# A third staging tile, the last pair's queries copied half by half, and the end of a unit issued behind the next unit's first scores, in a fused transformer block

## The chip, the cores and the metric

The kernel runs on one core of one Trainium2 chip. The metric is the device time of one execution in microseconds (us). The profile adds one execution seen by the hardware profiler: its engines are TensorE (PE), VectorE (DVE), ScalarE (ACT), GpSimd (POOL) and SyncE (SP), which issues the DMAs.

## The reference

One block of a streaming encoder, for 1024 tokens of width 1024, in float32. Heads have 64 columns; group A has 8 query heads over 2 key and value heads, group B has 8 heads of its own.

```
n = rms_norm(x); qa, ka, va, qb, kb, vb = split(n @ w_in)
ya = mixer_a(qa, ka, va)   # window of 3 chunks of 64, ALiBi, learned sinks
yb = mixer_b(qb, kb, vb)   # own chunk and 8 chunks before it, learned relative bias
h  = x + concat(rms_norm(ya), rms_norm(yb)) @ w_out
h  = h + relu(rms_norm(h) @ w_ff1)**2 @ w_ff2      # inner width 4096
out = rms_norm(h)
```

In mixer_b a token's scores are softmaxed over the keys of its band, and the softmax is multiplied by the values:

```
scores = einsum('bnqhd,bnshd->bnhqs', qc, kb) * HEAD_DIM ** -0.5 + bias
out = einsum('bnhqs,bnshd->bnqhd', softmax(where(valid, scores, -inf)), vb)
```

## The kernel before, in words

**Numbers.** Every float32 operand of a large product is kept as two pieces: a high part, a copy rounded to a shorter format by ScalarE, and a low part, the difference (`split_l`, L172, on VectorE or GpSimd). `mm3` multiplies high by high, high by low and low by high: three matmuls for one product (L166 is the matmul's line in the profile).

**Order.** Matmuls run in the order in which the code issues them: `pe` (L131) chains each to the one before. The other engines and SP each run their instructions in one fixed order too, but that one is set by a scheduler when the program is built, from what it estimates. A change of buffers or code can so move rows on ACT, DVE, POOL and SP. Every DMA that matters here is issued by SP, one after the other; an SP row that waits for its source holds all rows behind it.

**Buffers.** The pool `main` has three rings: 34 pages ("pg", `NPAGES`, 128 x 1024 float32 each), three weight stages ("ws") and two staging tiles ("tst", also 128 x 1024). Pages hold split weights, keys, queries, values, gated rows and later the operands of the MLP. A tile that is asked for waits until the earlier user of its buffer is done.

**Group B.** For each of four pairs of heads (j = 0 to 3) keys (kB), queries (qB) and values (vB) are projected, each in two halves of 512 tokens (t = 0, 1). `keys_b` (L391) handles keys and queries: VectorE scales the accumulator into the low tile `t1_..` (L398 queries, L400 keys), ScalarE casts the high tile `t0_..` (L401), GpSimd makes the low part in place (L172). Only after the second half the whole rows of both tiles, the high one first, are copied by DMA into the key pages KkB (L413, eight copies) and the query pages QqB (L410, four). High and low tile are one buffer of "tst" each, so with two buffers one projection fills the ring. `values_b` (L415) stages the values in "tst" as well (for the last pair in a page), splits them into two float16 pieces and transposes these by DMA (L446).

A `UnitB(pair, s, t)` is one head s of a pair for half the tokens, four blocks of 128. `first` holds its four scores: matmuls of QqB by KkB into `S_B`, a VectorE pass that adds the bias and finds the maximum `nm_B` (L607 for wide blocks, L609 for narrow), ScalarE's exponential (L610). Two blocks at a time then become float16 pieces `H_B` (ScalarE L850, VectorE L855) and are transposed by DMA into `G_B` (L858). `second` holds its products of `G_B` and the values into `av_B`; with the last of them `apply` (L868) adds the two halves of the accumulator, which hold the products of the values' two pieces, into `Y` (ScalarE L890, VectorE L891), and `finish` splits, squares and stores the result, gated by a power of two.

`interleave_b` (L1000) mixes one unit's products with the scores of a unit two further on (`LOOK_AHEAD`), and with steps of the `Filler` (L944): the projections of the next pair, or, at the end, `out_proj_a`. For the last pair `in_proj_halves` (L477) alternates queries and values by halves (q, v, q, v) and starts `out_proj_a` after the first two.

`out_proj_a` (L1015) multiplies group A's gated rows by w_out for eight blocks of tokens. `load_ya` (L928) loads a gated row `y0_m` (m = 0 to 3: one of four pairs of heads, first half of the tokens; L930) and splits it (ScalarE L897, VectorE L900). A block's result goes through a "tst" tile `o` (ScalarE L1039), is scaled there, and GpSimd adds it to the residual `h` that a DMA loads (L1040, L1026). Its steps are what TensorE does between the scores of the last pair.

**The MLP.** Both products use seven products of sums of quarter blocks in place of eight. Combinations of weights (T) are made by VectorE, cast by ScalarE (L1257) and split by GpSimd or VectorE into pages W; results are squared (L1307 Relu, L1308 Square) and stored. Tiles `k`, `v` and some rows come from "tst" too.

Of the kernel before, what the change touches and what calls it, by code (L numbers as in the profile page):

```python
# [8 lines left out]
F32 = mybir.dt.float32  # L9
# [19 lines left out]
BIG = 3e38  # L29
QA0, KA0, VA0, QB0, KB0, VB0 = 0, 512, 640, 768, 1280, 1792  # L30
WITH = ["", "", "k", "qv", "k", "qv", "k", "qv"]
NPAGES = 34
LOW_COLS = 256
GQ = 2
AHEAD1 = 2
# [18 lines left out]
def kernel(  # L54
# [288 lines left out]
    def place(acc, kind, name, dst, t, low_engine, st=None, rest=None):  # L343
        if kind == "v" and name != "vA":
            return values_b(acc, name, dst, t)
        if name[1] == "B":
            return keys_b(acc, kind, name, dst, t, low_engine)
        if st is not None:
            pass
        elif name == "vA":  # L350
            st = page([P, 2, HALF], f"ts_{name}_{t}")
        else:
            st = main.tile([P, 2, HALF], F32R, tag="tst", bufs=2, name=f"ts_{name}_{t}")
        c = slice(t * HALF, (t + 1) * HALF)
        if kind == "v":
            nc.vector.tensor_tensor(f(st[:, 0]), acc, R1[:, c], ALU.mult)
            return lambda *where: turn_v(st, name, dst, t, *where)
        if kind[0] == "q":
            nc.vector.scalar_tensor_tensor(f(st[:, 1]), acc, HD**-0.5, R1[:, c], ALU.mult, ALU.mult)
        else:  # L360
            nc.vector.tensor_tensor(f(st[:, 1]), acc, R1[:, c], ALU.mult)
        nc.scalar.activation(st[:, 0], f(st[:, 1]), AF.Copy)
        split_l(low_engine, st[:, 1], f(st[:, 1]), st[:, 0])

        def copies(heads):
            for hl in range(2):
                for s in heads:
                    src = f(st[s * HD : (s + 1) * HD, hl])
                    if kind == "q":
                        last = nc.sync.dma_start(f(dst[s][hl * HD : (hl + 1) * HD, c]), src)  # L370
                    else:
                        for rep in range(2):
                            last = nc.sync.dma_start(f(dst[2 * hl + s][rep * HD : (rep + 1) * HD, c]), src)
            return last.ins.name

        if rest is None:
            return copies(range(2))
        rest.append(lambda: copies((1,)))
        return copies((0,))
# [11 lines left out]
    def keys_b(acc, kind, name, dst, t, low_engine):  # L391

        if t == 0:
            halves[name] = [main.tile([P, SEQ], F32R, tag="tst", bufs=2, name=f"t{hl}_{name}") for hl in range(2)]
        c = slice(t * HALF, (t + 1) * HALF)
        hi, lo = (v[:, c] for v in halves[name])
        if kind == "q":
            nc.vector.scalar_tensor_tensor(f(lo), acc, HD**-0.5, R1[:, c], ALU.mult, ALU.mult)  # L398
        else:
            nc.vector.tensor_tensor(f(lo), acc, R1[:, c], ALU.mult)  # L400
        nc.scalar.activation(hi, f(lo), AF.Copy)  # L401
        split_l(low_engine, lo, f(lo), hi)
        if t == 0:
            return
        dst.extend(new_q(name) if kind == "q" else new_k(name))
        for hl, v in enumerate(halves[name]):
            for s in range(2):
                src = f(v[s * HD : (s + 1) * HD])
                if kind == "q":
                    nc.sync.dma_start(f(dst[s][hl * HD : (hl + 1) * HD]), src)  # L410
                else:
                    for rep in range(2):
                        nc.sync.dma_start(f(dst[2 * hl + s][rep * HD : (rep + 1) * HD]), src)  # L413

    def values_b(acc, name, dst, t):  # L415

        if t == 0:
            if name == "vB3":
                halves[name] = page([P, 2, HALF], f"ts_{name}", F32)
            else:  # L420
                halves[name] = main.tile([P, 2, HALF], F32, tag="tst", bufs=2, name=f"ts_{name}")
        st = halves[name]
        nc.vector.tensor_tensor(st[:, t], acc, R1[:, t * HALF : (t + 1) * HALF], ALU.mult)
        if t == 0:
            return
        st = st.rearrange("p a b -> p (a b)")
        top, e, up, down = (small.tile([P, 1], F32, tag=f"v{i}", bufs=2, name=f"{i}_{name}") for i in ("top", "e", "up", "down"))
        nc.vector.tensor_reduce(top, st, mybir.AxisListType.X, ALU.max, apply_absolute_value=True)
        nc.vector.tensor_scalar(top, top, 2.0**-90, None, ALU.max)
        nc.vector.tensor_scalar(e.bitcast(I32), top.bitcast(I32), 0xFF << 23, None, ALU.bitwise_and)  # L430
        nc.vector.tensor_scalar(
            up.bitcast(I32), e.bitcast(I32), -1.0, float((254 + V_UP) << 23), ALU.mult, ALU.add
        )
        nc.vector.tensor_scalar(
            down.bitcast(I32), e.bitcast(I32), 1.0, -float((V_UP + P_UP) << 23), ALU.mult, ALU.add
        )
        m = 4 + int(name[2:])
        gain = small.tile([P, 1], F32, tag="vgain", bufs=2, name=f"gain_{name}")
        nc.vector.tensor_tensor(gain, down, ogc[:, m : m + 1], ALU.mult)
        pieces = page([P, 2, SEQ], f"h{name}", F16)  # L440
        nc.scalar.activation(pieces[:, 0], st, AF.Copy, scale=up)
        nc.vector.scalar_tensor_tensor(pieces[:, 1], st, up, pieces[:, 0], ALU.mult, ALU.subtract)
        V = page([P, TB, 2, 2, HD], f"V{name}", F16)
        for s in range(2):
            for hl in range(2):
                nc.sync.dma_start_transpose(V[:, :, s, hl], pieces[s * HD : (s + 1) * HD, hl])  # L446
        dst.extend([V, down, gain])
# [341 lines left out]
            if self.i0 % 4 == 2:  # L789
                p.finish(self.i0 // 4)  # L790

    defer, pairs_b = [], []

    class UnitB:

# [72 lines left out]
        def apply(self, kb):  # L868
# [17 lines left out]
                    )  # L886
            if not last:
                return
            y = p.rows(self.t)[self.s * HD : (self.s + 1) * HD]
            nc.scalar.activation(y, self.av[HD:], AF.Copy)  # L890
            nc.vector.tensor_tensor(y, self.av[:HD], y, ALU.add)  # L891
# [108 lines left out]
    def interleave_b(unit, nexts, n_fill):  # L1000
# [3 lines left out]
        events = [(lead + (1 - lead) * r / rows, 1, r) for r in range(rows)]  # L1004
        events += [(NEXT_STEP[rows] * n, 0, n) for n in range(len(nexts))]
        spent = 0.0
        for at, kind, n in sorted(events):
            fill.steps(n_fill * (at - spent))
            spent = at
            (unit.second if kind else nexts)[n]()  # L1010
        fill.steps(n_fill * (1 - spent))
        while defer and not todo:
            defer.pop(0)[1]()

    def out_proj_a():  # L1015
# [5 lines left out]
        for tb in range(TB):  # L1021
# [6 lines left out]
            for n in range(8):  # L1028
# [6 lines left out]
                if last:  # L1035
                    yield
                if q == 3:
                    o = main.tile([P, HALF], F32, tag="tst", bufs=2, name=f"o{tb}_{dh}")
                    nc.scalar.activation(o, ps[dh], AF.Copy, scale=rA[:, tb : tb + 1])  # L1039
                    nc.gpsimd.tensor_tensor(h[:, c], h[:, c], o, ALU.add)  # L1040
                if not last:
# [68 lines left out]
        return mp.tile(shape, dt, tag="pg2", bufs=10, name=name)  # L1110

    def tst(shape, name):
        return main.tile(shape, F32, tag="tst", bufs=2, name=name)

    def pair_psum(name):
        return mps.tile([P, 2, HALF], F32, tag="ab", bufs=3, name=name)
# [19 lines left out]
    def rows2(tb):  # L1136
# [7 lines left out]
        nc.scalar.activation(h, ps, AF.Copy)  # L1144
        nc.sync.dma_start(hB[tb // 2][:, tb % 2], h)
        if tb % 4 < 2:
            rows[tb] = main.tile([P, 2, HALF], F32, tag="tst", bufs=2, name=f"n2_{tb}")
        else:
            rows[tb] = page([P, 2, HALF], f"n2_{tb}", F32)
        nc.vector.scalar_tensor_tensor(flat(rows[tb]), ps, r, g2b, ALU.mult, ALU.mult)  # L1150
# [510 lines left out]
```

## Time and profile before

| | |
|---|---|
| median of 3 runs | 1057.02 us (1054.84 to 1060.68) |
| the profiled execution | 1059.24 us |
| its span | 1057.5 us |
| mean granted TensorE clock | 0.990 |
| TensorE busy | 1024.0 us (97%) |
| VectorE, ScalarE, GpSimd busy | 700.8, 583.0, 425.0 us |
| moved by DMA | 183.77 MB |

Times of rows count from the start of the span. A row of the timeline gives the start, how long the group was busy, the engine, the source line, the instruction, the tile written and (after `<-`) the tiles read, their shape, and how many were taken together; in brackets stands how long the engine had been idle ahead, and what ended that. Tile names lose their numbers in the profile: `t_kB` is the high or the low tile of any pair. A stretch of a window row gives the window, its length, busy time and count by engine (PE, PE's weight loads, DVE, ACT, POOL), the granted clock, the mean busy share of the 16 DMA engines and GB/s. For SP a row's length is the time in which it issued.

By stages: the first projections and group A up to about 160, group B from there to 388, with the out-projection of group A among the last pair, and the MLP from about 450 to 1050, in which TensorE does not pause.

### The profile page before, as it was taken

To read this page: it belongs to the slowest core of one execution; us is meant where nothing else is said; L and a number is where in the kernel's file an instruction comes from. 1 tells how busy PE (TensorE), PEld (TensorE's weight loads), DVE (VectorE), ACT (ScalarE), POOL (GpSimd) and SP (SyncE) were. 2 spreads that over 40 slices of the span, in tenths; PEclk is the share of its full clock that TensorE was granted. 3 is DMA by queue.
4 is the path that set the end of the run, shared out by engine and by line. 5 is a ranking of instruction groups with operands and counts; after the bars stand their busy time and mean duration, and the time that the engine had idled before them with its cause. 6 is when DMAs were issued, how large, how long until landed. Compare 5 with 4: busy or idle time off the path is not lost.

```text
span 1057.5 us, 13848 instructions
## 1 busy us (share of the span) xinstructions
PE 1024.0 (97%) x4803; PEld 832.1 (79%) x4803; DVE 700.8 (66%) x1063; ACT 583.0 (55%) x969; POOL 425.0 (40%) x327
## 2 busy tenths in 40 slices
PE   9999998999958999999999999999999999999997
PEld 7888787767645768888888888888888888888886
DVE  6577677757674825795644535446869777678667
ACT  8666666756575756675554554455533333333347
POOL 0467565232461473306455444445015024024025
PEclk9999999999998999999999999999999999999999
DMA  9953537999999893315444534517997545533004
GB/s 358 261 149 91 134 86 172 193 209 201 200 257 213 177 312 116 120 55 177 170 140 155 182 117 145 194 60 257 371 393 264 168 127 170 177 124 100 1 1 159
DMA packets 141253, 183.77 MB, mean 174 GB/s; under 512 B 77952, under 2 KB 95360, under 8 KB 141184
## 3 DMA queue, kind: packets, MB, share of 16 engines
q1 hardware_dynamic: 141040, 182.63, 58.3%
q8 instruction: 38, 0.62, 0.2%
q14 instruction: 31, 0.25, 0.1%
q10 hardware_dynamic: 144, 0.26, 0.1%
HBM read 103.17 MB, written 42.99 MB: 138 GB/s over the span
## 4 chain that ended last, share of the span: by engine, by line
PE 56%; DVE 1%; ACT 0%; issue 0%; ACTq 0%
PE f L166 27%; PE f_a L166 16%; PE f_c L166 8%; PE f_b L166 4%; PE end L166 0%; DVE X L172 0%; DVE T L1235 0%; DVE k L1306 0%; ACT fo L147 0%; DVE S L1199 0%; DVE S L1206 0%; ACT uf L147 0%; DVE wf L147 0%; ACT C L147 0%; DVE S L1198 0%
## 5 line engine op out<-in xcount | busy, mean ns | idle before, releaser
L166 PE MATMUL f<-X,W 128*128 128x512 f32 x1344 | 305.8, 389 | 0.2 <-DVE X L172 0.2
L166 PEld LDWEIGHTS f<-X,W 128*128 128x128 f32 x1344 | 252.0, 188 | 52.8 <-DVE X L172 0.6
L166 PE MATMUL f_a<-V,U 128*128 128x512 f32 x756 | 173.5, 389 | 0.0
L172 POOL TENSOR_TENSOR U<-u,U 128x1024 fp32r<-128x1024 f32 x32 | 80.1, 2502 | 226.2 <-PE f_c L166 136.6
L166 PEld LDWEIGHTS f_a<-V,U 128*128 128x128 f32 x756 | 141.8, 188 | 29.7 <-DVE C L1550 0.3
L172 POOL TENSOR_TENSOR W<-T,W 128x1024 fp32r<-128x1024 f32 x29 | 77.0, 2655 | 122.9 <-ACT W L1257 122.9
L166 PE MATMUL f_c<-V,U 128*128 128x512 f32 x384 | 88.4, 389 | 0.0
L166 PEld LDWEIGHTS f_c<-V,U 128*128 128x128 f32 x384 | 72.1, 188 | 15.0
L1257 ACT ACTIVATE V<-Z 128x1024 fp32r<-128x1024 f32 x32 | 33.9, 1060 | 90.0 <-PE f_a L166 44.6
L172 POOL TENSOR_TENSOR W<-w,W 128x1024 fp32r<-128x1024 f32 x23 | 59.2, 2574 | 45.4 <-ACT W L1257 26.3
L1257 ACT ACTIVATE V<-w 128x1024 fp32r<-128x1024 f32 x24 | 25.4, 1060 | 79.3 <-issue 34.3
L1306 DVE TENSOR_TENSOR k<-f,k 128x1024 f32<-128x1024 f32 x24 | 29.3, 1222 | 60.0 <-PE f L166 60.0
L610 ACT ACTIVATE P_B<-P_B,nm_B 128x640 f32<-128x640 f32 (+2 forms) x64 | 44.3, 692 | 43.5 <-DVE nm_B L607 19.7
L1257 ACT ACTIVATE U<-u 128x1024 fp32r<-128x1024 f32 x56 | 58.5, 1045 | 11.8 <-DMA ud<-k 7.4
L172 DVE TENSOR_TENSOR V<-w,V 128x1024 fp32r<-128x1024 f32 x24 | 45.4, 1893 | 27.5 <-ACT V L1257 27.5
L855 DVE SCALAR_TENSOR_TENSOR H_B<-P_B,rc_B,H_B 128x640 f16<-128x640 f32 (+2 forms) x64 | 50.5, 813 | 17.4 <-ACT H_B L850 16.9
L166 PE MATMUL ip_qB<-nT,w_qB 128*128 128x512 f32 x192 | 56.4, 422 | 3.4 <-DVE t_qB L398 2.5
L166 PE MATMUL op_A<-w_o,y 128*128 128x512 f32 x192 | 57.4, 427 | 2.2 <-ACT o L1039 2.2
L166 PE MATMUL S_B<-KkB,QqB 128*128 128x320 f32 (+2 forms) x192 | 42.3, 330 | 15.5 <-DMA QqB<-t_qB 9.9
L166 PE MATMUL ip_kB<-nT,w_kB 128*128 128x512 f32 x192 | 53.5, 404 | 0.0
L1257 ACT ACTIVATE W<-w 128x1024 fp32r<-128x1024 f32 x24 | 25.3, 1059 | 47.4 <-PE f L166 25.4
L166 PE MATMUL ip_vB<-nT,w_vB 128*128 128x512 f32 x192 | 51.2, 400 | 0.0
(242 smaller groups left out, 1936.5 us busy)
## 6 DMA issues: line engine op xcount, KB each, us to landing
w<-in_w_ff_dram SPq DMA_DIRECT2D x64, 512.0 KB, 4.6
u<-ud SPq DMA_DIRECT2D x56, 512.0 KB, 4.3
ud<-k SPq DMA_DIRECT2D x48, 512.0 KB, 4.7
KkB<-t_kB SPq DMA_DIRECT2D x32, 256.0 KB, 4.7
xr<-in_x_dram SPq DMA_DIRECT2D x8, 512.0 KB, 9.1
QqB<-t_qB SPq DMA_DIRECT2D x16, 256.0 KB, 4.8
st_o<-in_w_out_dram SPq DMA_DIRECT2D x8, 512.0 KB, 5.5
h<-in_x_dram SPq DMA_DIRECT2D x8, 512.0 KB, 4.7
```

Source lines behind the costliest of these rows:

```text
L166: pe(nc.tensor.matmul(*args, **kw))
L172: return engine.tensor_tensor(lo, full, f(hi), ALU.subtract)
L610: nc.scalar.activation(pr, pr, AF.Exp, bias=nm, scale=-1.0, accum_out=sm)
L855: nc.vector.scalar_tensor_tensor(lo, q, rc, hi, ALU.mult, ALU.subtract)
L1257: nc.scalar.activation(w[0], full, AF.Copy)
L1306: dve.tensor_tensor(v, ps, v, ALU.add)
```

## The change

Five things are edited. The page ring shrinks from 34 to 33, and the staging ring grows from two tiles to three. In `keys_b` the low tile is asked for ahead of the high one, and its copies stand first. For the last pair's queries alone (qB3) each half is copied as soon as it is split: four copies of 64 x 512 after t = 0 and four after t = 1, in place of four of 64 x 1024. The closing steps of a unit of group B (ScalarE's and VectorE's `Y`, `finish`) move from `apply` to a new `end`, which `interleave_b` calls behind the first event of the next call, the first score of a coming unit; for the last unit, with its own last product.

```diff
-NPAGES = 34
+NPAGES = 33
+TST = 3
...
         if t == 0:
-            halves[name] = [main.tile([P, SEQ], F32R, tag="tst", bufs=2, name=f"t{hl}_{name}") for hl in range(2)]
+            halves[name] = [main.tile([P, SEQ], F32R, tag="tst", bufs=TST, name=f"t{hl}_{name}") for hl in (1, 0)]
         c = slice(t * HALF, (t + 1) * HALF)
-        hi, lo = (v[:, c] for v in halves[name])
+        lo, hi = (v[:, c] for v in halves[name])
...
-        if t == 0:
-            return
-        dst.extend(new_q(name) if kind == "q" else new_k(name))
-        for hl, v in enumerate(halves[name]):
+        split = name == "qB3"
+        if t == 0 or not split:
+            if t == 0 and not split:
+                return
+            dst.extend(new_q(name) if kind == "q" else new_k(name))
+        c = c if split else slice(0, SEQ)
+        for hl, v in zip((1, 0), halves[name]):
             for s in range(2):
-                src = f(v[s * HD : (s + 1) * HD])
+                src = f(v[s * HD : (s + 1) * HD, c])
                 if kind == "q":
-                    nc.sync.dma_start(f(dst[s][hl * HD : (hl + 1) * HD]), src)
+                    nc.sync.dma_start(f(dst[s][hl * HD : (hl + 1) * HD, c]), src)
...
             if not last:
                 return
+            ends.append(self.end)
+
+        def end(self):
+            p = self.pair
             y = p.rows(self.t)[self.s * HD : (self.s + 1) * HD]
...
-        for at, kind, n in sorted(events):
+        for k, (at, kind, n) in enumerate(sorted(events)):
             fill.steps(n_fill * (at - spent))
             spent = at
             (unit.second if kind else nexts)[n]()
+            if ends and (k == 0 or unit is units[-1][0] and k == len(events) - 1):
+                ends.pop()()
```

The other lines of the diff replace `bufs=2` by `bufs=TST` where "tst" is asked for. Code behind the first edit moves down by 1 to 10 lines (L172 becomes L173, L410 L414, L858 L862, L930 L938).

TensorE's order is the same before and after. On SP, from the keys of the last pair to the probabilities of unit B5_1 (head 5, second half of the tokens), before (G_B5_0 is a transpose of that unit's probabilities, y0_m a load of a gated row, st_om of a part of w_out):

```order
L413 DMA KkB32_3219<-t1_kB3_3132 64x1024 x2
L413 DMA KkB33_3220<-t1_kB3_3132 64x1024 x2
L858 DMA_TRANSPOSE G_B5_0_3165<-H_B5_0_3_3243 128x14x128
...
L858 DMA_TRANSPOSE G_B4_1_3276<-H_B4_1_1_3314 128x20x128
...
L930 DMA y0_2_3420<-ya_87 128x512
L122 DMA st_o4_4157<-in_w_out_dram 128x1024
L858 DMA_TRANSPOSE G_B4_1_3276<-H_B4_1_3_3365 128x20x128
L930 DMA y0_3_3434<-ya_87 128x512
L122 DMA st_o5_4171<-in_w_out_dram 128x1024
L410 DMA QqB30_3517<-t0_qB3_3301 64x1024
...
L858 DMA_TRANSPOSE G_B5_1_3445<-H_B5_1_1_3476 128x20x128
```

and after:

```order
L414 DMA QqB30_3306<-t1_qB3_3301 64x512
L414 DMA QqB31_3307<-t1_qB3_3301 64x512
L414 DMA QqB30_3306<-t0_qB3_3302 64x512
L414 DMA QqB31_3307<-t0_qB3_3302 64x512
L862 DMA_TRANSPOSE G_B4_1_3269<-H_B4_1_1_3320 128x20x128
...
L862 DMA_TRANSPOSE G_B4_1_3269<-H_B4_1_3_3371 128x20x128
L938 DMA y0_2_3423<-ya_87 128x512
L123 DMA st_o4_4158<-in_w_out_dram 128x1024
L123 DMA st_o5_4172<-in_w_out_dram 128x1024
L862 DMA_TRANSPOSE G_B5_1_3448<-H_B5_1_1_3482 128x20x128
L938 DMA y0_3_3437<-ya_87 128x512
L414 DMA QqB30_3306<-t1_qB3_3301 64x512
```

The first half's copies stand ahead of both transposes of G_B4_1, the second half's behind the first of G_B5_1; y0_2 and y0_3 have each moved behind one transpose of 20 blocks.

On ScalarE, around the exponentials of unit B5_1 and the first one of the last pair (B6_0; w0_o3 is the high part of a piece of w_out, Y6_0 the closing copy of a unit), before:

```order
L222 ACTIVATE w0_o3_3425<-st_o3_3424 128x512 x2
L610 ACTIVATE P_B5_1_1_3468,sm_B5_1_3443<-P_B5_1_1_3468,nm_B5_1_3442 128x640
L897 ACTIVATE y0_2_3420<-y0_2_3420,ogc_82 128x512
L610 ACTIVATE P_B5_1_2_3492,sm_B5_1_3443<-P_B5_1_2_3492,nm_B5_1_3442 128x640
L401 ACTIVATE t0_qB3_3301<-t1_qB3_3302 128x512
L890 ACTIVATE Y6_0_3374<-av_B5_0_3480 64x512
L850 ACTIVATE H_B5_1_1_3476<-P_B5_1_0_3447,rc_B5_1_3444 128x640
L850 ACTIVATE H_B5_1_1_3476<-P_B5_1_1_3468,rc_B5_1_3444 128x640
L897 ACTIVATE y0_3_3434<-y0_3_3434,ogc_82 128x512
```

and after:

```order
L854 ACTIVATE H_B5_1_1_3482<-P_B5_1_1_3474,rc_B5_1_3447 128x640
L905 ACTIVATE y0_1_3409<-y0_1_3409,ogc_82 128x512
L402 ACTIVATE t0_qB3_3302<-t1_qB3_3301 128x512
L223 ACTIVATE w0_o3_3428<-st_o3_3427 128x512 x2
L898 ACTIVATE Y6_0_3464<-av_B5_0_3486 64x512
L614 ACTIVATE P_B5_1_3_3530,sm_B5_1_3446<-P_B5_1_3_3530,nm_B5_1_3445 128x640
L905 ACTIVATE y0_2_3423<-y0_2_3423,ogc_82 128x512
L854 ACTIVATE H_B5_1_3_3539<-P_B5_1_2_3498,rc_B5_1_3447 128x640
L854 ACTIVATE H_B5_1_3_3539<-P_B5_1_3_3530,rc_B5_1_3447 128x640
L614 ACTIVATE P_B6_0_0_3598,sm_B6_0_3594<-P_B6_0_0_3598,nm_B6_0_3593 128x128
L905 ACTIVATE y0_3_3437<-y0_3_3437,ogc_82 128x512
```

The casts of y0_2 and y0_3 have moved back, y0_3 behind the last pair's first exponential; the pieces H_B5_1_1 stand earlier.

On ScalarE again, in the second column block of the MLP's first product (k0_6 is a result of the first block, W1_50 the high part of the fifth combination of weights of the second), before:

```order
L1300 ACTIVATE k0_6_4995<-f1_0_1_4771 128x1024
L1178 ACTIVATE X401_4998<-F21_4713 128x2x256 x2
L1257 ACTIVATE W1_50_5011<-T1_5_5009 128x1024
L1307 ACTIVATE k0_6_4995<-k0_6_4995 128x1024
L1308 ACTIVATE k0_6_4995<-k0_6_4995 128x1024
L1257 ACTIVATE W0_40_5045<-T0_4_5043 128x1024
```

and after:

```order
L1310 ACTIVATE k0_6_4999<-f1_0_1_4775 128x1024
L1188 ACTIVATE X401_5002<-F21_4717 128x2x256 x2
L1317 ACTIVATE k0_6_4999<-k0_6_4999 128x1024
L1318 ACTIVATE k0_6_4999<-k0_6_4999 128x1024
L1267 ACTIVATE W1_50_5015<-T1_5_5013 128x1024
L1267 ACTIVATE W0_40_5049<-T0_4_5047 128x1024
```

The cast of W1_50 has moved behind the Relu and the Square of k0_6.

More of the change, by code (lines that the diff above doesn't have):

```diff
@@ L352, in place @@
         else:
-            st = main.tile([P, 2, HALF], F32R, tag="tst", bufs=2, name=f"ts_{name}_{t}")
+            st = main.tile([P, 2, HALF], F32R, tag="tst", bufs=TST, name=f"ts_{name}_{t}")
         c = slice(t * HALF, (t + 1) * HALF)
@@ L420, in values_b @@
             else:
-                halves[name] = main.tile([P, 2, HALF], F32, tag="tst", bufs=2, name=f"ts_{name}")
+                halves[name] = main.tile([P, 2, HALF], F32, tag="tst", bufs=TST, name=f"ts_{name}")
         st = halves[name]
@@ L790, in apply @@
                 p.finish(self.i0 // 4)
-    defer, pairs_b = [], []
+    defer, pairs_b, ends = [], [], []
     class UnitB:
@@ L1037, in out_proj_a @@
                 if q == 3:
-                    o = main.tile([P, HALF], F32, tag="tst", bufs=2, name=f"o{tb}_{dh}")
+                    o = main.tile([P, HALF], F32, tag="tst", bufs=TST, name=f"o{tb}_{dh}")
                     nc.scalar.activation(o, ps[dh], AF.Copy, scale=rA[:, tb : tb + 1])
@@ L1112, in tst @@
     def tst(shape, name):
-        return main.tile(shape, F32, tag="tst", bufs=2, name=name)
+        return main.tile(shape, F32, tag="tst", bufs=TST, name=name)
     def pair_psum(name):
@@ L1146, in rows2 @@
         if tb % 4 < 2:
-            rows[tb] = main.tile([P, 2, HALF], F32, tag="tst", bufs=2, name=f"n2_{tb}")
+            rows[tb] = main.tile([P, 2, HALF], F32, tag="tst", bufs=TST, name=f"n2_{tb}")
         else:
```

## The prediction

> **What bounds the kernel now.** I read the page first, then TensorE's waits, its timeline around each wait, the granted clock by stretch, and last the engines and the queue that end those waits.
>
> ```profile
> span 1057.5 us, 13848 instructions
> ...
> PE 1024.0 (97%) x4803; PEld 832.1 (79%) x4803; DVE 700.8 (66%) x1063; ACT 583.0 (55%) x969; POOL 425.0 (40%) x327
> ```
>
> TensorE is busy 1024.0 of 1057.5 us, so all its pauses together are 33.5 us, and the change leaves every matmul in its place. It can win only pauses, and what the clock loses behind them. The profiled execution took 1059.24 us (1.7 us lie outside its span), 2.2 us above the median of the runs, 1057.02. The sum below is made against 1059.24 and carried over to the median. I call 0.5%, 5.3 us, the least that a measurement of this kernel tells from no change. The larger waits of TensorE, as "engine, waiting tile, what ended the wait: total us, times, longest":
>
> ```profile
> PE S_B L166 <- DMA QqB<-t_qB: 9.9, 1, 9.9
> PE S_B L166 <- DVE nm_B L607: 2.9, 2, 1.9
> PE S_B L166 <- DVE nm_B L609: 2.7, 3, 1.4
> ...
> PE av_B L166 <- DMA G_B<-H_B: 0.4, 1, 0.4
> ```
>
> One wait is nearly a third of all idle time: scores that wait for queries copied by DMA. TensorE's timeline has the places (start, busy us, instruction, count, idle before it and its releaser):
>
> ```profile
> 123.19 0.38 PE L166 MATMUL av_A<-T_A,VA 128*128 128x256 f32 x1 [1.62 <-ACT T_A L617]
> ...
> 230.31 3.80 PE L166 MATMUL ip_qB<-nT,w_qB 128*128 128x512 f32 x9 [1.87 <-DVE t_qB L398]
> ...
> 318.97 0.77 PE L166 MATMUL S_B<-KkB,QqB 128*128 128x256 f32 x2 [9.88 <-DMA QqB<-t_qB]
> 319.54 2.76 PE L166 MATMUL op_A<-w_o,y 128*128 128x512 f32 x6
> ...
> 326.07 0.86 PE L166 MATMUL op_A<-w_o,y 128*128 128x512 f32 x3
> ...
> 338.06 0.96 PE L166 MATMUL op_A<-w_o,y 128*128 128x512 f32 x3 [2.24 <-ACT o L1039]
> ```
>
> The pauses cost more than their length. By 10 us, with the granted clock behind POOL's column:
>
> ```profile
> 120.00:130.00 10.00, 8.04 (x35) 6.32 (x33) 5.81 (x18) 6.32 (x18) 5.27 (x5) 0.83 0.17 57
> ...
> 230.00:240.00 10.00, 9.69 (x41) 7.53 (x41) 6.00 (x15) 6.17 (x11) 4.98 (x16) 0.83 1.02 231
> ...
> 300.00:310.00 10.00, 8.06 (x38) 5.88 (x36) 7.93 (x12) 6.74 (x13) 8.22 (x12) 1.00 1.07 259
> 310.00:320.00 10.00, 1.03 (x4) 0.96 (x5) 6.74 (x11) 3.94 (x7) 1.94 (x2) 0.60 1.07 252
> 320.00:330.00 10.00, 10.00 (x45) 6.90 (x43) 6.50 (x24) 7.67 (x17) 0.29 (x2) 0.89 0.94 215
> ...
> 340.00:350.00 10.00, 10.00 (x44) 6.96 (x44) 8.52 (x13) 7.76 (x16) 4.68 (x4) 0.86 0.91 151
> ```
>
> Busy time by (1 - clock) is the loss: 8.04 x 0.17 = 1.4 us behind the pause at 123, 9.69 x 0.17 = 1.6 at 230, 0.4 + 1.1 = 1.5 behind the long one, 10 x 0.14 = 1.4 behind 338. Where the clock stayed at 1.00, as in 300 to 310, nothing is added.
>
> [...]
>
> **The third staging tile.** Keys and queries of group B are staged in a pair of tiles, which the next projection needs back. With two tiles it waits until the DMA copies have landed. SP, ScalarE and VectorE show it:
>
> ```profile
> 108.30 7.31 SPq L413 DMA_DIRECT2D KkB<-t_kB  x8
> ```
> ```profile
> 120.62 0.63 ACT L401 ACTIVATE t_qB<-t_qB 128x512 fp32r<-128x512 f32 x1 [3.79 <-DMA KkB<-t_kB]
> ...
> 290.27 0.63 ACT L401 ACTIVATE t_qB<-t_qB 128x512 fp32r<-128x512 f32 x1 [1.99 <-DMA KkB<-t_kB]
> ```
> ```profile
> 229.56 0.69 DVE L398 SCALAR_TENSOR_TENSOR t_qB<-ip_qB,R 128x512 f32<-128x512 f32 x1 [2.42 <-POOL w_vB L172]
> ...
> 285.83 0.69 DVE L398 SCALAR_TENSOR_TENSOR t_qB<-ip_qB,R 128x512 f32<-128x512 f32 x1 [3.30 <-DMA KkB<-t_kB]
> ```
>
> The eight key copies occupy SP for 7.31 us. With three tiles the queries' low part takes the free one at once, and only the high part waits, for the tile copied first, half of those 7.31 us earlier. Against that, the low keys now go out first and wait for GpSimd's split of half a tile (about 1.3 us, the row at 290.98 below). So some 3.7 - 1.3 = 2.4 us of ScalarE's stall of 3.79 go, and TensorE's pause there, 1.62, fits under it. At 123: 1.62 + 1.4 = 3.0 gained (bounds 1.0 and 3.4, with a second pause of 0.34 that follows). At 230 VectorE's stall of 2.42 goes whole: 1.87 + 1.6 = 3.5 at most; I take 3.0, since ScalarE's next stall then comes earlier. The two waits for "nm_B L607", 2.9 in all at clock 1.00, lie behind the stalls at 285 and 290: 2.4 gained (bounds 1.0 and 2.9).
>
> At 338 it is the tile of the out-projection's rows. GpSimd frees them only after the residual has landed:
>
> ```profile
> 336.02 2.49 POOL L1040 TENSOR_TENSOR h<-h,o 128x512 f32<-128x512 f32 x2 [11.90 <-DMA h<-in_x_dram]
> ```
>
> A third tile lets one more row leave its accumulator. But TensorE will come earlier, and the residual's load stands behind transposes on SP. Of 2.24 + 1.4 = 3.6 I take 2.8 (0 to 3.6).
>
> **The last queries by halves.** Their first half has been ready since GpSimd's split at 290.98; the second is split at 309.41; all copies go after it:
>
> ```profile
> 290.98 1.30 POOL L172 TENSOR_TENSOR t_qB<-t_qB,t_qB 128x512 fp32r<-128x512 f32 x1 [4.97 <-ACT t_qB L401]
> ...
> 309.41 1.26 POOL L172 TENSOR_TENSOR t_qB<-t_qB,t_qB 128x512 fp32r<-128x512 f32 x1
> ```
> ```profile
> 294.17 3.06 SPq L858 DMA_TRANSPOSE G_B<-H_B  x1
> ...
> 301.12 6.37 SPq L858 DMA_TRANSPOSE G_B<-H_B  x1
> 307.61 0.69 SPq L930 DMA_DIRECT2D y<-ya  x1
> ...
> 311.34 1.63 SPq L410 DMA_DIRECT2D QqB<-t_qB  x2
> ```
>
> The first scores read only the first half. In the new order its four copies stand behind the key copies, ahead of the transposes issued at 294.17; they can land soon after 300, and TensorE wants them at 318.97 - 9.88 = 309.1. So 9.88 goes, and the clock's 1.5: 11.4.
>
> What is late next stands on the same queue. Before, the fourth gated row (y<-ya) was issued at 307.61; now it stands behind one more transpose of 20 blocks, and so behind the third gated row and two weight loads: 301.12 + 6.37 + about 1.3 = 308.8, then the transpose, 3.06 to 6.37, so 311.9 to 315.2. The landing:
>
> ```profile
> q1 hardware_dynamic: 34386, 23.05, 95.3%
> ...
> y<-ya SPq DMA_DIRECT2D x8, 256.0 KB, 6.0
> ```
>
> The median landing of 6.0 (from 290 to 390; I allow 3.5) and about 1.5 for its split give 316.9 to 322.7. TensorE read that row at 326.07, which is 7.1 after the first score; without the 1.2 lost at a low clock, 5.9, so now at 315.0. That is a new wait of 2 to 8 us; I take 5.0 with its clock. The place nets 11.4 - 5.0 = 6.4. Four more copies at SP's 0.5 to 0.8 us each lie in time that the second half has to spare, being read a unit of scores later.
>
> **The end of a unit, deferred.** ScalarE's and VectorE's copy of the result (about 0.6 us each) now stands behind the next unit's first score. It adds nothing; it may shorten the 2.7 us of "nm_B L609". The accumulator has two buffers and is wanted back a unit later. I take 0 (0 to 2.7 gained).
>
> **The lost page.** Splits wait longer for a page. Two come late. The low part of a key weight:
>
> ```profile
> 138.29 2.83 POOL L172 TENSOR_TENSOR w_kB<-st_kB,w_kB 128x256 fp32r<-128x256 f32 x4
> ```
>
> ```profile
> 143.42 1.52 PE L166 MATMUL ip_vB<-nT,w_vB 128*128 128x512 f32 x6
> ...
> 144.92 0.94 PE L166 MATMUL ip_kB<-nT,w_kB 128*128 128x512 f32 x3
> ```
>
> Its page now comes from the values' projection, which ends at 143.42 + 1.52 = 144.9 at the latest; the third matmul of the second row reads it at 144.92 + 0.6 = 145.5. One piece of 2.83 / 4 = 0.7 has to come first: with the engines' hand-over 0.3 late. And one weight combination at the first MLP products: its cast now stands behind a Relu and a Square.
>
> ```profile
> 477.96 1.06 ACT L1308 ACTIVATE k<-k 128x1024 f32<-128x1024 f32 x1
> ```
> ```profile
> 475.64 2.41 POOL L172 TENSOR_TENSOR W<-T,W 128x1024 fp32r<-128x1024 f32 x1 [29.70 <-ACT W L1257]
> ```
> ```profile
> 459.50 32.71 PE L166 MATMUL f<-X,W 128*128 128x512 f32 x143 [0.16 <-DVE X L172]
> ```
>
> The cast runs at about 479.0, the split ends at 479.0 + 1.06 + 2.41 = 482.5 instead of 478.05. Its first reader is the 90th matmul of the last row, at 0.228 us each 479.8, and its low part is read at 480.3. If ScalarE's two steps stay where they are, 2.2 late; if they come a microsecond earlier, 1.0. I take 1.5. Other weights are ready early. This one is read at 496.1, by the same count of matmuls:
>
> ```profile
> 484.84 1.04 ACT L1257 ACTIVATE W<-w 128x1024 fp32r<-128x1024 f32 x1
> ```
>
> That is 10 us ahead, nearly two products of 24 x 0.228 = 5.5 us, and one page less costs at most one of them.
>
> **The end of attention.** The transposed probabilities of the last units (av_B, 0.4 late already) have no slack, and the queue's engines are 95.3% busy from 290 to 390. What TensorE wins before it partly waits here: 2.0 (0 to 5).
>
> **The sum.** -3.0 - 3.0 - 2.4 - 2.8 - 6.4 + 0.3 + 1.5 + 2.0 = -13.8. From 1059.24 that is 1045.4, from the median 1043.2; I forecast 1044.0. With the kinder bounds together (-3.4, -3.5, -2.9, -3.6, -9.4, -2.7, and 0.3 and 1.0 back) it would be 24 us, with the harsher ones (-1.0, -1.5, -1.0, 0, -3.4, +0.3, +2.2, +5.0) nothing. Neither set comes whole.
>
> **Rivals.** (1) The DMA queue takes over. If its engines are full at 95.3%, the 100 us from 290 on can shrink by their free 4.7 us, instead of 6.4 + 2.8 - 2.0 = 7.2; and if the same holds from 200 on, the 3.0 and 2.4 are lost too: 1044.0 + 2.5 + 5.4 = 1051.9. For it speaks that row; against it, that at shares of 0.91 and 1.07 those engines moved 151 and 259 GB/s in the windows shown, so that the share does not tell what they can move. 0.16.
> [...]
>
> (2) The half does not get out. The copies of the low part stand first and hold SP until GpSimd has split it; if GpSimd is held by weight splits, or the transposes pass first, the 9.88 stays, and 1044.0 + 6.4 = 1050.4 comes, up to 1052.8 where the 2.4 of the waits at 285 and 290 stays too. The idle 4.97 ahead of GpSimd's split at 290.98 speaks against it. 0.07.
>
> (3) Slower: pages run out in the MLP. If a cast behind Relu and Square stands in TensorE's way not once but for two of seven products in each of eight column blocks, 16 x 2.2 = 35 us come, less 1.5 counted: 1044.0 + 33.7 = 1078. It decides once the slip exceeds the 10 us ahead; one product of 5.5 stays short of that. 0.06.
>
> **The numbers.** The forecast has 0.71. Faster by over 0.5% (below 1051.7): the forecast nearly whole, 0.69, over half of (1), 0.09, and over half of (2), 0.04: 0.82. Slower: 0.06, rival (3). Same: the rest, 0.12. The range goes down to 1036, two thirds of the way from the sum to the kinder bounds, and up to 1053, past rivals (1) and (2); no more than 0.2 is left out.
>
> **What would show it.** The row "S_B <- DMA QqB" gone from the waits, and op_A waiting for its gated row (y) some 6 us behind the first score of the last pair; no stall on KkB ahead of t_qB near 120; clock 1.00 from 120 to 130; a wait of f for W near 480, and for none later. Wrong: 9.88 still there, or G_B waits of over 5 us before 390, or waits for W in every column block.

## The result, and the profile after

The changed kernel took 1049.70 us (median of 5, 1049.25 to 1049.82) beside 1056.84 for the kernel before. The ratio on record is 0.9921, with a 95% interval of 0.9904 to 0.9938 (the two medians alone would give 0.9932; with five runs of each, either is within it). A second measurement, on another chip (below, e12), gave 0.9911 (0.9899 to 0.9923). That is 7.1 to 9.4 us faster; 13 had been forecast. The two profiled executions differ by 1059.24 - 1049.81 = 9.4 us, of which 2.3 lie in how far the two stand above their medians (2.4 and 0.1). In the comparisons below one execution, of 5869.56 us in e1, is left out of the ratio as a slow one.

The page after, and TensorE's waits:

```profile
span 1048.0 us, 13827 instructions
...
PE 1022.3 (98%) x4803; PEld 829.6 (79%) x4803; DVE 711.9 (68%) x1063; ACT 581.5 (55%) x969; POOL 426.0 (41%) x327
```
```profile
PE op_A L167 <- DVE ts_vB L427: 4.7, 1, 4.7
PE op_A L167 <- ACT o L1049: 3.9, 2, 2.2
PE S_B L167 <- DVE nm_B L611: 2.6, 4, 1.7
PE S_B L167 <- DVE nm_B L613: 1.4, 1, 1.4
PE f L167 <- POOL W L173: 1.1, 1, 1.1
```

The wait for the copied queries is gone, and with it those of ip_qB for t_qB. At the head stands a wait that the kernel before did not have: op_A for the staging of values.

TensorE runs the same matmuls in the same order, so one and the same row can be looked up in both traces, and the difference of its starts tells how far ahead the changed kernel is there. Before, two rows that were not shown yet:

```profile
301.89 0.85 PE L166 MATMUL S_B<-KkB,QqB 128*128 128x320 f32 x4 [1.03 <-DVE nm_B L607]
...
388.36 8.45 PE L166 MATMUL op_B<-w_o,y 128*128 128x512 f32 x36 [0.17 <-ACT o L1039]
```

and after:

```profile
293.25 0.85 PE L167 MATMUL S_B<-KkB,QqB 128*128 128x320 f32 x4 [0.21 <-DVE nm_B L611]
...
300.29 0.40 PE L167 MATMUL S_B<-KkB,QqB 128*128 128x256 f32 x2
305.39 2.93 PE L167 MATMUL op_A<-w_o,y 128*128 128x512 f32 x6 [4.71 <-DVE ts_vB L427]
...
316.43 0.96 PE L167 MATMUL op_A<-w_o,y 128*128 128x512 f32 x3 [1.69 <-ACT o L1049]
...
323.84 0.86 PE L167 MATMUL op_A<-w_o,y 128*128 128x512 f32 x3
...
330.87 0.98 PE L167 MATMUL op_A<-w_o,y 128*128 128x512 f32 x3 [2.16 <-ACT o L1049]
...
376.20 4.15 PE L167 MATMUL op_B<-w_o,y 128*128 128x512 f32 x17 [0.17 <-ACT o L1049]
```

| the same row | before | after | ahead by |
|---|---|---|---|
| scores of unit B5_1 | 301.89 | 293.25 | 8.6 |
| first score of the last pair | 318.97 | 300.29 | 18.7 |
| the op_A behind it | 319.54 | 305.39 | 14.2 |
| op_A of the third block | 338.06 | 323.84 | 14.2 |
| first op_B | 388.36 | 376.20 | 12.2 |
| end of the span | 1057.5 | 1048.0 | 9.5 |

So the last pair's first score gains 10 us, of which 4.5 are lost at the next row; another 2.0 go between 338.06 and the first op_B, and 2.7 from there to the end, 1.6 of them at two waits in the MLP (1.08 for W at 469.35, 0.54 for k at 730.89).

What holds the row at 305.39 stands on VectorE. It is an accumulator: the out-projection has two, and the second one still holds the last values, which VectorE empties (ts_vB) only after what it has in front of it. After, VectorE:

```profile
300.48 0.81 DVE L611 CUSTOM_DVE_ANT_0 P_B<-S_B,b_B 128x640 f32<-128x640 f32 x1
...
301.22 1.02 DVE L908 SCALAR_TENSOR_TENSOR y<-y,ogc 128x512 fp32r<-128x512 f32 x1
302.27 0.68 DVE L899 TENSOR_TENSOR Y<-av_B,Y 64x512 f32<-64x512 f32 x1
...
303.64 1.09 DVE L908 SCALAR_TENSOR_TENSOR y<-y,ogc 128x512 fp32r<-128x512 f32 x1
304.66 0.68 DVE L427 TENSOR_TENSOR ts_vB<-ip_vB,R 128x512 f32<-128x512 f32 x1
```

No row here waits: VectorE is simply busy. Before the change it did this work while TensorE stood still for 9.88 us:

```profile
312.08 0.68 DVE L423 TENSOR_TENSOR ts_vB<-ip_vB,R 128x512 f32<-128x512 f32 x1
```

On ScalarE, two casts of gated rows wait for their loads, with the finished rows of the out-projection (o) behind them:

```profile
311.09 0.72 ACT L905 ACTIVATE y<-y,ogc 128x512 fp32r<-128x512 f32 x1 [4.22 <-DMA y<-ya]
...
328.21 0.72 ACT L905 ACTIVATE y<-y,ogc 128x512 fp32r<-128x512 f32 x1 [2.56 <-DMA y<-ya]
...
330.15 0.67 ACT L1049 ACTIVATE o<-op_A,rgA 128x512 f32<-128x512 f32 x1
```

By windows, the clock (behind POOL's column) is 1.00 where the pauses of 123 and 230 are gone, and 0.83 in the windows of two of the new ones:

```profile
120.00:130.00 10.00, 10.00 (x59) 8.57 (x59) 7.54 (x25) 6.92 (x19) 10.00 (x12) 1.00 0.67 191
230.00:240.00 10.00, 10.00 (x53) 8.03 (x52) 7.84 (x17) 7.46 (x12) 5.10 (x13) 1.00 1.08 214
300.00:310.00 10.00, 5.29 (x20) 4.03 (x20) 8.67 (x17) 5.07 (x10) 5.32 (x5) 0.83 1.05 237
...
330.00:340.00 10.00, 9.13 (x40) 6.72 (x41) 8.85 (x16) 7.99 (x16) 5.54 (x5) 0.83 1.07 238
```

The pause of 2.16 cost 9.13 x 0.17 = 1.6 us more in this execution. It shows in the rows: the second and third group of three op_A behind the pause, at 331.89 and 333.36, took 1.36 and 1.63 us. That does not follow from the pause's length: in e12, the same kernel, the same pause was 2.72 us and these two groups took 0.99 and 0.94 us, and in e9 (below) it was 3.73 us, with 0.99 and 0.94 too. What decides whether the clock falls behind a pause is not shown by these runs.

### The profile page after: what moved, and what is told of

Read it like the earlier page. It is cut to its first block, busy times and chain, and to the rows that moved or that the text cites. A ratio compares the mean times of both kernels' runs of the same rounds, so it can differ in the third digit from the quotient of the medians.

```text
span 1048.0 us, 13827 instructions
## 1 busy us (share of the span) xinstructions
PE 1022.3 (98%) x4803; PEld 829.6 (79%) x4803; DVE 711.9 (68%) x1063; ACT 581.5 (55%) x969; POOL 426.0 (41%) x327
## 4 chain that ended last, share of the span: by engine, by line
PE 58%; issue 4%; DVE 1%; ACT 1%; DMA 1%; POOL 0%; ACTq 0%; DVEq 0%; POOLq 0%
PE f L167 24%; PE f_a L167 16%; PE f_c L167 8%; PE op_B L167 4%; PE f_b L167 4%; DMA G_B<-H_B 1%; POOL W L173 0%; PE tp L170 0%; DVE V L173 0%; DVE Z L1245 0%; DVE T L1245 0%; PE end L167 0%; PE op_A L167 0%; DVE k L1316 0%; PE ss_B L167 0%
## 5 line engine op out<-in xcount | busy, mean ns | idle before, releaser
L173 POOL TENSOR_TENSOR U<-u,U 128x1024 fp32r<-128x1024 f32 x32 | 80.1, 2502 | 224.9 <-PE f_c L167 135.0
L173 POOL TENSOR_TENSOR W<-T,W 128x1024 fp32r<-128x1024 f32 x29 | 76.4, 2636 | 103.3 <-ACT W L1267 91.2
L173 POOL TENSOR_TENSOR W<-w,W 128x1024 fp32r<-128x1024 f32 x23 | 59.5, 2587 | 68.8 <-ACT W L1267 62.9
L1267 ACT ACTIVATE W<-T 128x1024 fp32r<-128x1024 f32 x32 | 33.9, 1059 | 66.2 <-PE f L167 26.4
L173 DVE TENSOR_TENSOR V<-w,V 128x1024 fp32r<-128x1024 f32 x24 | 48.9, 2039 | 28.0 <-ACT V L1267 24.6
L167 PE MATMUL ip_qB<-nT,w_qB 128*128 128x512 f32 x192 | 53.8, 406 | 1.1 <-DVE t_kB L401 1.0
```

Source lines behind the costliest of these rows:

```text
L167: pe(nc.tensor.matmul(*args, **kw))
L173: return engine.tensor_tensor(lo, full, f(hi), ALU.subtract)
L1267: nc.scalar.activation(w[0], full, AF.Copy)
```

## The experiments: one part at a time

The question is whether the 9 us come from the halves, from the third tile or from the deferred end, each by itself, or only from parts together, and what takes back the rest of the 13. The letters are those of the expectations, which say what each theory holds there. Four kernels take one part of the change each, on one chip, beside the kernel before (1058.45 us there).

**e1, halves alone.** The edit is that of the change, with the high tile first:

```diff
-        if t == 0:
-            return
-        dst.extend(new_q(name) if kind == "q" else new_k(name))
+        split = name == "qB3"
+        if t == 0 or not split:
+            if t == 0 and not split:
+                return
+            dst.extend(new_q(name) if kind == "q" else new_k(name))
+        c = c if split else slice(0, SEQ)
...
```

> The kernel before with one part alone: the last pair's queries (qB3) copied half by half, the high tile first as before, two staging tiles, 34 pages, a unit's end where it was. Theory A (the wait of 9.88 us goes with the halves, but most of it comes back because VectorE and ScalarE hold accumulators of the out-projection some us later): 3 to 5 us faster than before, the row S_B <- DMA QqB gone, a wait of op_A of 3 us or more in the 20 us behind the first score of the last pair. Theory B (the pause goes whole, nothing is handed back there): 10 to 11.5 us faster. Theory C (the half is early only with three tiles): within 1 us of before, the wait of over 8 us still there.

1058.47 us, ratio 0.9999 (0.9988 to 1.0011): no gain. By time that is C's, by the trace A's first step: the wait for the copy is gone, and a wait of op_A of 3.04 us stands behind the first score. TensorE in e1:

```profile
309.64 0.40 PE L166 MATMUL S_B<-KkB,QqB 128*128 128x256 f32 x2
...
313.07 1.65 PE L166 MATMUL op_A<-w_o,y 128*128 128x512 f32 x6 [3.04 <-DVE ts_vB L426]
...
318.03 0.61 PE L166 MATMUL S_B<-KkB,QqB 128*128 128x384 f32 x2 [1.28 <-DVE nm_B L612]
...
321.40 0.73 PE L166 MATMUL S_B<-KkB,QqB 128*128 128x512 f32 x2 [1.48 <-DVE nm_B L612]
...
336.54 1.65 PE L166 MATMUL op_A<-w_o,y 128*128 128x512 f32 x3 [4.82 <-ACT o L1042]
```

The first score stands 9.3 us earlier than before, while the row of 301.89 stands 0.7 later (302.57): 10.0 won. Of the last wait 2.24 stood there before, so the four waits hand back 3.04 + 1.28 + 1.48 + 4.82 - 2.24 = 8.4; the row at 336.54 is 1.5 ahead, the first op_B 0.8. The last of the four, on ScalarE, GpSimd and SP:

```profile
335.80 0.69 ACT L1042 ACTIVATE o<-op_A,rgA 128x512 f32<-128x512 f32 x1 [2.73 <-POOL h L1043]
```
```profile
334.50 2.49 POOL L1043 TENSOR_TENSOR h<-h,o 128x512 f32<-128x512 f32 x2 [11.55 <-DMA h<-in_x_dram]
```
```profile
330.23 0.52 SPq L1029 DMA_DIRECT2D h<-in_x_dram  x1
```

The residual's load is issued at 330.23 (331.55 before): it comes only 1.3 us earlier.

**e2, the third tile alone** (33 pages, high first, whole copies):

```diff
-NPAGES = 34
+NPAGES = 33
+TST = 3
...
```

with `bufs=TST` for "tst".

> The kernel before with 33 pages and three staging tiles alone, the high tile asked for and copied first, queries copied whole. Theory A (the third tile takes away the pauses near 123 and 230 with the clock's loss behind them, 3.8 + 3.1 us by the two traces, and the page costs 1 to 2): 4 to 7 us faster, the wait of S_B for DMA QqB still 8 to 11 us. Theory B (what is won before 300 is waited for at the copy of the last queries, whose time the queue sets): within 1.5 us of before, that wait 4 us longer than 9.9.

1060.21 us, ratio 1.0016 (1.0005 to 1.0027), slower by a little. By time this is close to B's number; the wait for the copy, 10.88 instead of 9.88, is as A has it, not 4 us longer. In the trace the pauses near 123 and 230 are gone, as A has it too: TensorE is 6.8 us ahead at the row of 294.94, and 3.5 of that are left at the last pair's first score. But this profiled execution took 1057.41, 2.8 us less than the median of e2, so its places say little.

**e3, the deferred end alone** (the edits of `apply`, `end` and `interleave_b`).

> The kernel before with the end of a unit of group B behind the next unit's first score, and nothing else. Theory A (this is what took away the waits for nm_B L609 near 262 and 274, 2.4 us of the shift between the two traces): 1 to 3 us faster, those waits gone. Theory B (those went with the third tile or by chance of the order): within 1 us of before, those waits still there.

1059.67 us, ratio 1.0012 (1.0000 to 1.0025): no gain, 1.2 us slower where B allowed 1. Of the two waits, that near 274 is gone and that near 262 is still there (0.44); the profiled execution of e3 took 1063.03, 3.4 us above its median.

**e4, the lost page alone** (`NPAGES = 33`).

> The kernel before with 33 pages instead of 34 and nothing else: the price of the third tile. Theory A (one late weight combination near 470 and one near 730): 1 to 2.5 us slower, a wait of f for W of about 1 us. Theory B (the lost page is where most of the missing gain went): 4 us slower or more, with new waits before 400.

1066.33 us, ratio 1.0073 (1.0059 to 1.0087): 7.7 us slower, B's number. The waits of scores on the rows that stand between 257 and 275 before, 1.33 us together there (0.43 and 0.90), are 3.42, these three and one of 0.74:

```profile
261.02 0.50 PE L166 MATMUL S_B<-KkB,QqB 128*128 128x256 f32 x2 [0.42 <-DVE nm_B L607]
...
263.87 0.62 PE L166 MATMUL S_B<-KkB,QqB 128*128 128x384 f32 x2 [0.78 <-DVE nm_B L609]
...
267.23 0.73 PE L166 MATMUL S_B<-KkB,QqB 128*128 128x512 f32 x2 [1.48 <-DVE nm_B L609]
```

Which page comes late there, and how it reaches VectorE, was not followed up. In the MLP the two waits of the changed kernel are here as well (1.09 for W, 0.56 for k). All ten traces with 33 pages have them, and none of the four with 34. What follows: none of these parts gains anything when it is added alone; the medians of e1, e2 and e3 against 1058.45 add up to 0.0 + 1.8 + 1.2 = 3.0 us slower (e2 has e4's page in it), and together they are 7 to 9 faster. The third tile, once the page is given up, is worth 1066.33 - 1060.21 = 6.1 us. The low tile first was not tried alone.

## The experiments: one part left out

Three kernels leave one part out of the change; a fourth gives e1 the tile that it lacked (kernel before: 1059.25 us).

**e5, the end not deferred** (`ends.append(self.end)` and the head of `end` taken out).

> The changed kernel with the end of a unit put back behind its last product; halves, three tiles, 33 pages and the low tile first stay. Theory A (halves and the third tile need each other, since with two tiles the pause of 9.9 us only moves to the rows of the out-projection, as the run with halves alone showed; the deferred end adds little): within 2 us of the changed kernel, so 5 to 7 us faster than before. Theory B (all four edits are needed, because the scheduler's order is good in just that combination): no more than 3 us faster than before.

1049.72 us, ratio 0.9911 (0.9892 to 0.9930), as the changed kernel (0.9911 in e12): A, though it is 9.4 us faster than before by the ratio, where A had said 5 to 7. The deferred end carries nothing that these intervals could show.

**e6, queries copied whole:**

```diff
-        split = name == "qB3"
+        split = False
```

> The changed kernel with the last queries copied whole again; the rest of the change stays. Theory A (halves are worth some 10 us where three tiles are there): 1 us faster to 3 us slower than before, the wait of S_B for DMA QqB of 8 us or more back. Theory B (the third tile and the deferred end carry the gain): 5 us or more faster than before.

1054.26 us, ratio 0.9955 (0.9939 to 0.9970): 4.8 us faster than before, between the two. TensorE in e6:

```profile
312.36 0.76 PE L167 MATMUL S_B<-KkB,QqB 128*128 128x256 f32 x2 [12.65 <-DMA QqB<-t_qB]
```

This row stood at 318.97, so the copies come 6.6 us earlier; TensorE is there 318.97 - 9.88 - (312.36 - 12.65) = 9.4 us earlier and waits the rest. Against e5 on the same chip (0.9911, the change without its deferred end) the halves are worth 1054.26 - 1049.72 = 4.5 us.

**e7, the high tile first** in three tiles:

```diff
-    for hl in (1, 0)]
+    for hl in (0, 1)]
...
-        for hl, v in zip((1, 0), halves[name]):
+        for hl, v in enumerate(halves[name]):
```

> The changed kernel with the high tile asked for and copied first, as before; the rest of the change stays. Theory A (which tile goes first matters little): within 2 us of the changed kernel. Theory B (the tile whose buffer is freed first decides ScalarE's stall on KkB, and with it the pauses near 123 and 230): 3 us or more slower than the changed kernel, pauses of 1.5 us or more near 123 or 230.

1054.37 us, ratio 0.9953 (0.9936 to 0.9970), some 4.5 us slower than the changed kernel. By time that is B, but not for B's reason; the pauses near 123 and 230 stay away. These have come or grown:

```profile
171.40 0.66 PE L170 MATMUL pt_A<-ident,P_A 128*128 128x128 f32 x4 [2.14 <-DVE T_A L173]
```
```profile
307.91 2.93 PE L167 MATMUL op_A<-w_o,y 128*128 128x512 f32 x6 [5.87 <-DVE ts_vB L427]
...
316.22 0.73 PE L167 MATMUL S_B<-KkB,QqB 128*128 128x512 f32 x2 [1.91 <-DVE nm_B L613]
```

The edit changes the scheduler's order of several engines at once, so whether the freed buffer or the order does it stays open.

Beside e2 (three tiles and 33 pages, neither halves nor the low tile first: 1.0016) e6 and e7 say more, if the deferred end is taken as nothing: with the third tile there, the low tile first alone brings 0.9955 and the halves alone 0.9953, both 0.9911. Each is worth some 6.5 us without the other and 4.5 beside it. (e2 was compared with the kernel before on another chip.)

**e8, halves and a buffer for o:**

```diff
-o = main.tile([P, HALF], F32, tag="tst", bufs=2, name=f"o{tb}_{dh}")
+o = main.tile([P, HALF], F32, tag=("tst", "os")[dh], bufs=2 - dh, name=f"o{tb}_{dh}")
```

> Halves alone (34 pages, two staging tiles, high first, ends where they were), but every second row of the out-projection of group A gets a buffer of its own, so that three such rows can wait for their residual and no page is given up. Theory A (the third buffer for these rows is what the halves lack): 3 us or more faster than before, the wait of 4.8 us for o near 336 gone or under 2.5 us. Theory B (something else holds TensorE there, the row's place in ScalarE's order or the late gated rows): within 1.5 us of halves alone, which equalled the kernel before.

1055.45 us, ratio 0.9971 (0.9958 to 0.9984): 3.1 us faster than before where halves alone gave nothing. That is A. The wait of 4.82 for o at that row is gone, and one of 3.02 stands at a later row of o:

```profile
340.61 1.65 PE L166 MATMUL op_A<-w_o,y 128*128 128x512 f32 x3 [3.02 <-ACT o L1042]
```

So the halves gain only where the out-projection's rows have a third buffer. That is shown by the times of e1 and e8, which differ in that line alone, and again by e2 against e7; the trace of e8 is of an execution of 1058.0 us, 2.6 above its median. The buffer for o without the halves was not run.

## The experiments: can the new waits be taken away?

Three kernels force the order of an engine at one place each, and e12 is the changed kernel itself (kernel before: 1058.37 us). Nothing is computed otherwise.

**e9**: VectorE stages the values ahead of the low parts of y0_1 and y0_2.

```diff
...
+        if name == "vB3":
+            behind_of["vB3"] = staged.ins.name
+            for work in lows:
+                behind(work(), "vB3")
...
```

The lines left out also hold the cast of y0_3 behind the first exponential of the last pair, where it stands in the changed kernel.

> The changed kernel, with VectorE's order alone forced at one place: the low parts of the gated rows y0_1 and y0_2 stand behind the staging of the last values' second half (ts_vB) instead of ahead of it, and the low part of y0_3 behind one exponential pass more. Theory A (the 4.7 us pause of op_A is an accumulator that VectorE empties late, because it works through its queue): that pause shrinks by 1.5 to 2.5 us, the time by 1 to 2. Theory B (what is won there is waited for at the next rows, which come by the DMA queue): the pause shrinks, the time stays within 0.7 us of the changed kernel.

**e10**: ScalarE moves o1_1 out ahead of the casts of y1.

```diff
...
+                    if (tb, dh) == (Y1_AT, 1):
+                        behind_of["o"] = moved.ins.name
+                        for work in turns_y:
+                            work()()
...
```

> The changed kernel, with ScalarE's order forced at one place: the casts of the second half's gated rows (y1_0 to y1_3), which wait for their loads, stand behind the out-projection row o1_1 instead of y1_0 and y1_1 ahead of it. Theory A (the 2.2 us pause of op_A near 331 is ScalarE waiting for a load with the finished row behind it): that pause goes, 2 to 3.5 us faster than the changed kernel with the clock's loss. Theory B (the transposes and the residual's load set the pace from there to 380): within 0.7 us of the changed kernel, a wait for G_B or for o later instead.

**e11**: both.

> Both orders forced: the staging of the values ahead of the gated rows on VectorE, and the row o1_1 ahead of the casts of y1 on ScalarE. Theory A: the two gains add up, 3 to 5 us faster than the changed kernel. Theory B: within 1 us of the better of the two alone.

**e12**: the changed kernel.

> The changed kernel itself, on the chip of these runs, as the measure for the three: 7 to 9 us faster than before by either theory, its first pause behind the last pair's first score 4 to 5 us.

| | us | ratio to before | 95% interval |
|---|---|---|---|
| e9 | 1049.40 | 0.9918 | 0.9905 to 0.9932 |
| e10 | 1049.49 | 0.9916 | 0.9900 to 0.9933 |
| e11 | 1048.93 | 0.9909 | 0.9894 to 0.9924 |
| e12 | 1048.95 | 0.9911 | 0.9899 to 0.9923 |

All four are alike: B (e12 gains 9.4 us, a little more than the 7 to 9 expected). Each wait did shrink as it was meant to. In e9 TensorE waits 2.76 for ts_vB instead of 4.71 (4.6 in e12), 1.9 less, and then for the gated row y0_3, for o, and at the end for transposed probabilities:

```profile
303.71 1.65 PE L174 MATMUL op_A<-w_o,y 128*128 128x512 f32 x6 [2.76 <-DVE ts_vB L436]
...
311.46 1.29 PE L174 MATMUL op_A<-w_o,y 128*128 128x512 f32 x3 [1.02 <-ACT y L924]
...
331.09 0.96 PE L174 MATMUL op_A<-w_o,y 128*128 128x512 f32 x3 [3.73 <-ACT o L1076]
...
370.46 0.48 PE L174 MATMUL av_B<-G_B,VvB 128*128 128x384 f16 x2 [0.71 <-DMA G_B<-H_B]
```

In e10 the pause near 331 is gone, and waits for scores (0.68), o (0.91) and G_B stand later:

```profile
338.03 0.85 PE L175 MATMUL S_B<-KkB,QqB 128*128 128x320 f32 x4 [0.68 <-DVE nm_B L619]
...
359.40 0.96 PE L175 MATMUL op_A<-w_o,y 128*128 128x512 f32 x3 [0.91 <-ACT o L1062]
...
371.51 0.48 PE L175 MATMUL av_B<-G_B,VvB 128*128 128x384 f16 x2 [1.00 <-DMA G_B<-H_B]
```

and SP in e10 shows what comes last there, four transposes of 20 blocks with a few loads between them, and VectorE the pass behind which the fourth is issued:

```profile
346.47 13.67 SPq L870 DMA_TRANSPOSE G_B<-H_B  x3
...
362.56 6.90 SPq L870 DMA_TRANSPOSE G_B<-H_B  x1
```
```profile
360.86 1.68 DVE L867 SCALAR_TENSOR_TENSOR H_B<-P_B,rc_B,H_B 128x640 f16<-128x640 f32 x2 [0.17 <-ACT H_B L862]
```

From 346.47 to the end of the fourth are 362.56 + 6.90 - 346.47 = 23.0 us, and the row av_B starts 2.05 us later. It is much the same in the kernel before, the changed one, e9, e11 and e12: 23.1 to 23.5 us, then 2.05 to 2.12. In e11 the wait for G_B is 1.39, in e12 1.06. What is won between the first of these transposes and av_B is therefore waited for at G_B.

It is not SP's queue that sets this pace. In all six traces each of the four is issued within 0.1 us of the end of VectorE's pass that makes its pieces H_B (here 360.86 + 1.68 = 362.54), and the row of three counts SP's waits for these passes in; the three take 3.35, 3.67 and 3.06 us by themselves. VectorE's own waits from 343 to 361 (0.17 to 1.05 us) are all for ScalarE. So the probabilities come at the pace of these two engines, and only the last transpose, 6.90 us, is SP's own. What decides when the first of the four can start was not followed up, so why the gains ahead of it are not kept is open in part; the rows above show some of them waited for at y, o and the scores.

None of the versions beats the changed kernel by more than its measurement is uncertain.

## Why the prediction was partly right

**Right in direction and in most places.** By 302, -3.0, -3.0 and -2.4 were forecast, 8.4 in all; the same row stands 8.6 earlier. The clock's loss behind short pauses, taken from the rows, came back where they went (1.00 in place of 0.83 from 120 to 130 and from 230 to 240). ScalarE's stall on KkB near 120 is gone, as forecast. The weight combination was forecast 1.5 late and waits 1.08 (below); the wait of 0.54 for k was not forecast. The end's deferral was taken at 0, and e5 against e12 shows 0.

```profile
469.35 10.99 PE L167 MATMUL f<-X,W 128*128 128x512 f32 x47 [1.08 <-POOL W L173]
```

**Right sum by 302, wrong make-up.** The waits of scores near 285 to 302 hardly went: 2.9 in two before, 2.6 in four after. ScalarE's stall on the key copies grew there:

```profile
280.03 0.63 ACT L402 ACTIVATE t_qB<-t_qB 128x512 fp32r<-128x512 f32 x1 [3.55 <-DMA KkB<-t_kB]
```

It was 1.99. The low keys going out first are not the cause: with three tiles and the high keys first it is 3.37 (e2) and 3.67 (e7). The 2.4 forecast there became nothing. In their place more was won than forecast at 123 (4.1 for 3.0) and at 230 (3.6 for 3.0), 1.9 near 262 and 274, where the waits of scores went, and 1.6 near 171 to 175; 1.4 were lost before 120 and 1.0 from 145 to 163, where 0.3 had been forecast. That the sum agrees so well is luck. The waits near 262 and 274 are gone in e5 as well, which has no deferred end: they did not go by that.

**The step that failed: "The place nets 11.4 - 5.0 = 6.4".** The 11.4 were nearly right: 18.7 - 8.6 = 10.1 at the row, and the clock's loss behind the long pause on top. What came back is read from a row further on: the same op_A stands at 328.15 before and at 316.43 after, 11.7 ahead. The place nets 11.7 - 8.6 = 3.1, so 11.4 - 3.1 = 8.3 were handed back in place of 5.0, in the pauses of 4.71 and 1.69 and in the clock behind the first.

```profile
328.15 1.05 PE L166 MATMUL op_A<-w_o,y 128*128 128x512 f32 x3
```

The step named the fourth gated row, and ScalarE does wait 4.22 for it, though it was issued at 307.27 and not at 311.9 to 315.2, since SP's rows ahead of it had come earlier too:

```profile
307.27 0.52 SPq L938 DMA_DIRECT2D y<-ya  x1
```

But its lateness lies hidden under a pause that I had not looked for: the accumulator behind VectorE's queue. The row was there: before, VectorE emptied it at 312.08, three us after TensorE had stopped at 309.1, which cost nothing only because TensorE stood still. The 2.8 for 338 became some 0.4: the pause of 2.24 went (11.7 ahead became 14.2), and one of 2.16 with its clock, at 330.87 after, left 12.2 by the first op_B.

In the prediction's terms 8.6 were won for 8.1 by 302 (8.4 less the 0.3 of the key weight), 3.1 for 6.4 at the place, 0.4 for 2.8 at 338; at the end of attention 0 were lost for 2.0, and in the MLP 2.7 for 1.5. That is 9.4 for 13.8.

**What that shows.** The 2.0 that I set aside for the end of attention was not lost there in the changed kernel: TensorE's wait for G_B, 0.36 before, is 0.10 there. It is the bound that e9 to e11 meet. The first rival, that the queue takes over, is not what they show: loads that stand behind transposes on SP come late (ScalarE waits 4.22 and 2.56 for gated rows), but the last transposes themselves wait for VectorE.

**The baseline.** The sum was made against an execution that lay 2.4 us above its median and carried to the median whole. Against its own execution the change gave 9.4 of the 13.8, against the median 7.1. The kernel before varies from 1054.55 to 1061.61 over all its executions on record, the changed one from 1048.51 to 1050.06 in ten executions; that a part of its pauses comes and goes was not followed up.

The rival of the lost page came nowhere near its price in the whole change (1.08 at the first MLP products). That the page costs 7.7 us by itself (e4) was in none of the cases; in the changed kernel its price is not known beyond the two waits of 1.6 us.

## What to carry to other kernels

A long wait of the bounding engine is also the time in which the others catch up, as VectorE did in the kernel before: it emptied the accumulator at 312.08, within TensorE's 9.88 us. Before counting it as a gain, list what each in-order engine still has to do at the moment when the wait would have ended, and which buffer the next instruction needs from it. And a change whose parts gain nothing one by one can still gain together (here 0.0, 1.8 and 1.2 us slower in e1, e2 and e3, and 7.1 to 9.4 faster together), when each takes away the wait that would have followed the other's; so leave parts out as well as trying them alone.

## What had not been expected of the hardware

Transposes of the same size held SP for very different times. In the changed kernel three of the last four of 20 blocks took 3.66, 3.63 and 3.07 us and the fourth 7.43; before, one at 294.17 took 3.06 and one at 301.12 took 6.37. A row that counts several together, such as that of 13.67 in e10, also holds the waits between them. A load behind a transpose on SP was issued only when SP had done with that (at 369.25 in the changed kernel, 0.1 after the end of the fourth). Nothing here tells how much of the longer times is the transposes' own rate and how much the other traffic: the DMA engines' busy share in the changed kernel was 1.04 from 340 to 350, 0.80 from 350 to 360 and 1.04 from 360 to 370.
